# Five of eleven pairs of row tiles of each down product by Strassen's algorithm as well

## The chip, the cores and the metric

One core of a Trainium2 chip. The metric is the device time in microseconds of one execution of the whole program, the median of several runs. Matrix products run on TensorE (PE), elementwise work on VectorE (DVE) and ScalarE (ACT), a little on GpSimd (POOL); nearly all DMAs are issued by SyncE (SP), whose queue is worked through in order.

## The reference

Two decoder layers over 512 tokens of width 1024, in fp32. Each layer has two feed-forward blocks (FFN), so there are four:

```python
D_MODEL = 1024
D_FF = 2816
def swiglu(x, w_gu, w_down):
    gate, up = jnp.split(x @ w_gu, 2, axis=-1)
    return (jax.nn.silu(gate) * up) @ w_down
# per layer
#   h += 0.5 * post(SwiGLU_1(pre(h)))
#   h += post(concat(A, B, C) @ W_out)          "mix"
#   h += 0.5 * post(SwiGLU_2(pre(h)))
#   h += post((p[i] @ W_ple) * sigmoid(pre(h) @ W_gate))   "ple"
```

`pre` and `post` are RMS norms with gains. The down product is 512x2816 times 2816x1024.

## The kernel before

Every fp32 operand is split into two fp32r parts, hi (a cast, on ACT) and lo (operand minus hi, on DVE), and each product of two tiles is three matmuls into one PSUM bank: hi·hi, hi·lo, lo·hi (`mm3`, L252 to L254). So each weight tile of 128x1024 costs a load into `wst` (two buffers), an ACT cast `whi` (L143) and a DVE subtraction `wlo` (L140).

The gate/up product is already done by the Strassen–Winograd scheme: 7 products instead of 8 (`step`, L382; M1 to M7) for each of 11 pairs of row tiles, called mp 0 to 10 (mp 0 in the plain way). M4 of a pair is held back behind M2 of the next pair. From the products DVE and ACT assemble `c11`, `c12`, `c22`, then silu and product give g, whose last half is L455; g (128x1024: two row tiles of 512 tokens) goes to DRAM as `gd[mp]` (`store`, L406).

The down product then runs over k = 0 to 21, the 22 row tiles of 128 of the inner dimension. For each even k a pair of g is loaded back as `gl` (L543), cast to `gh` (ACT, L544) and reduced to its lo part (DVE, L545); for each k a weight tile is loaded and split. Then 4 token tiles t times 2 halves n times 3 matmuls of 128x512 go into the eight banks `acc[t, n]`, so all eight PSUM banks sum over the whole of k. The last TAIL = 4 values of k are done one token tile after the other. While t = 3 finishes, t = 0 and 1 go through `post_tile` (norm and residual; its DVE steps are L200, L199, L204) and `pre_tile` (the next norm, `v`, `hn` L228), and `turn` transposes them into `hT` (PE L234, ACT L237, DVE L238); t = 2 and 3 follow at the start of the next phase (`chains`), among its first weight splits (`wlo`, or `uw` in ple).

Each engine runs its instructions in the order in which the program has them; SP does so with its DMAs. A DMA into a buffer waits until the buffer's last reader is done, and all that stands behind it on SP waits too. Tiles called T, O, Q, U in the change and `gl`, `gh` share pools by tags: "u" and "s" and "x" of four buffers of 128x1024, "z" of five.

Of the kernel before, what the change touches and what calls it, by code (L numbers as in the profile page):

```python
# [21 lines left out]
P = 128  # L22
# [51 lines left out]
def kernel(ctx: ExitStack, tc: tile.TileContext, a: dict, out: bass.AP, phases=None):  # L74
# [210 lines left out]
    def ffn(l, w_gu, w_down, i, ends, hook):  # L285
# [140 lines left out]
        def step(mp, name, kind, w):  # L426
# [80 lines left out]
        held = (1, "M4", A22, w4)  # L507

        while True:
            prefetch(LOOK - len(queue))  # L510
            if not queue:
                break
            x = queue.pop(0)
            if x[:2] == (5, "M2"):
                hook(0)
            if x[1] == "M4" and x[0] < NMP - 1:
                held = x
                continue
            if x[1] == "M4":
                step(*held)  # L520
            step(*x)
# [4 lines left out]
        accs = {}  # L526
        ws, gs = {}, {}

        def down(t, k):
            for n in range(2):  # L530
                if not k:
                    accs[t, n] = ps(f"acc{t}{n}", ORD[t])
                mm3(accs[t, n][:], cut(gs[k], tsl(t)), ws[k](n * 512), k == 0, False)

        for k in range(KF):
            if k == 4:
                gpost, npre = ends()
            if k == 6:
                hook(1)
            ws[k] = load_w(w_down[k * P:(k + 1) * P, :])  # L540
            if k % 2 == 0:
                gl, gh = ut("gl", "z", F32R), ut("gh", "z", F32R)
                nc.sync.dma_start(gl[:].bitcast(F32), gd[k // 2][:])  # L543
                nc.scalar.copy(gh[:], gl[:].bitcast(F32))  # L544
                nc.vector.tensor_tensor(out=gl[:], in0=gl[:].bitcast(F32), in1=gh[:].bitcast(F32), op=ALU.subtract)  # L545
            gs[k] = tuple(x[:, (k % 2) * 512:(k % 2 + 1) * 512] for x in (gh, gl))
            if k < KF - TAIL:
                for t in range(NT):
                    down(t, k)
        def parts(t):  # L550
            return [accs[t, n][:] for n in range(2)]

        for t in range(NT):
            tail = [(n, k) for n in range(2) for k in range(KF - TAIL, KF)]
            if t == NT - 1:
# [802 lines left out]
```

## Time and profile before

| | |
|---|---|
| median of 3 runs | 2006.47 us (2005.75 to 2008.36) |
| profiled execution, its own time | 2007.29 us |
| its span in the trace | 2005.5 us (1.8 us lie outside) |
| granted TensorE clock, mean | 0.995 |
| PE busy | 1948.8 us, 97% |
| DVE busy | 1398.2 us, 70% |
| ACT busy | 925.4 us, 46% |
| first FFN: gate/up, down | 15.8 to 249.5 us, 249.5 to 371.5 us |

A busy PE is a PE that has matmuls in flight, and the duration of one matmul in a row is its time through the array; how fast matmuls follow each other is read from the starts of successive rows.

### The profile page before, as it was taken

What the parts mean: (1) busy time and instruction counts of PE and PEld (TensorE: products, weight loads), DVE (VectorE), ACT (ScalarE), POOL (GpSimd) and SP (SyncE); (2) the same over time, 40 slices, a digit from 0 to 9 for tenths busy, and PEclk for the clock granted to TensorE, in tenths of its full rate; (3) what the DMA queues carried; (4) which work ended last, traced back from release to release, by engine and by line L of the source; (5) the groups of instructions that cost most, each with busy time, mean ns of one, the idle gap of its engine ahead of it and who ended that gap; (6) DMA issues with size and microseconds to landing.
All of it is one profiled execution on the core that took longest, in us unless ns stands there. A gap on an engine that the chain in (4) does not pass through costs nothing.

```text
span 2005.5 us, 31044 instructions
## 1 busy us (share of the span) xinstructions
PE 1948.8 (97%) x12524; PEld 1754.2 (87%) x12524; DVE 1398.2 (70%) x2058; ACT 925.4 (46%) x1463; POOL 112.7 (6%) x135
## 2 busy tenths in 40 slices
PE   7999999999999999999999999999999999999988
PEld 6999988788689999887799999887877899998866
DVE  6887753669879888435688886346797798874364
ACT  4544433555545444324455444236545555443242
POOL 1000000113100000000000000001140000000000
PEclk9999999999999999999999999999998999999999
DMA  5543364323324342643253434443142244336431
GB/s 156 157 144 117 130 216 147 105 67 108 120 64 141 112 149 94 210 142 100 74 158 106 154 126 155 160 137 116 55 130 64 69 143 145 119 105 213 145 110 48
DMA packets 160609, 251.17 MB, mean 125 GB/s; under 512 B 11473, under 2 KB 116817, under 8 KB 160465
## 3 DMA queue, kind: packets, MB, share of 16 engines
q1 hardware_dynamic: 158160, 244.99, 38.0%
q10 hardware_dynamic: 2304, 4.20, 0.6%
q8 instruction: 98, 1.61, 0.3%
q14 instruction: 47, 0.38, 0.1%
HBM read 217.17 MB, written 29.36 MB: 123 GB/s over the span
## 4 chain that ended last, share of the span: by engine, by line
PE 79%; DVE 13%; ACT 3%; DMA 2%; issue 2%; POOL 1%; SPq 0%; DVEq 0%; ACTq 0%; POOLq 0%
PE X L382 21%; PE Z L382 11%; PE acc L254 8%; PE acc L252 8%; PE acc L253 8%; PE Y L382 5%; DVE wlo L140 2%; PE gate L253 1%; PE gate L254 1%; PE gate L252 1%; PE wo L252 1%; DVE A L321 1%; PE wo L254 1%; POOL r L181 1%; PE wo L253 1%
## 5 line engine op out<-in xcount | busy, mean ns | idle before, releaser
L337 ACT CAST whi<-wraw 128x1024 fp32r<-128x1024 f32 x280 | 291.9, 1050 | 342.1 <-issue 153.2
L140 DVE TENSOR_TENSOR wlo<-wraw,whi 128x1024 fp32r<-128x1024 f32 x280 | 339.7, 1221 | 93.5 <-ACT whi L337 93.1
L140 DVE TENSOR_TENSOR wlo<-wst,whi 128x1024 fp32r<-128x1024 f32 x150 | 183.2, 1222 | 150.5 <-ACT whi L143 150.0
L254 PE MATMUL acc<-whi,gl 128*128 128x512 f32 x704 | 274.5, 390 | 1.5 <-DVE gl L545 1.5
L252 PE MATMUL acc<-whi,gh 128*128 128x512 f32 x704 | 274.5, 390 | 0.0
L253 PE MATMUL acc<-wlo,gh 128*128 128x512 f32 x704 | 273.9, 389 | 0.0
L143 ACT CAST whi<-wst 128x1024 fp32r<-128x1024 f32 x150 | 157.4, 1050 | 212.5 <-PE acc L254 97.5
L382 PE MATMUL X<-hT,whi 128*128 128x256 f32 x1280 | 233.7, 283 | 0.0
L382 PEld LDWEIGHTS X<-hT,whi 128*128 128x128 f32 x1280 | 199.7, 192 | 0.0
L342 DVE TENSOR_TENSOR wraw<-wraw 128x1024 f32<-128x1024 f32 x160 | 195.4, 1222 | 3.4
L382 PE MATMUL X<-hT,wlo 128*128 128x256 f32 x640 | 181.1, 283 | 0.0
L254 PEld LDWEIGHTS acc<-whi,gl 128*128 128x128 f32 x704 | 132.1, 188 | 30.5 <-DVE gl L545 3.1
L253 PEld LDWEIGHTS acc<-wlo,gh 128*128 128x128 f32 x704 | 132.2, 188 | 27.2
L252 PEld LDWEIGHTS acc<-whi,gh 128*128 128x128 f32 x704 | 132.2, 188 | 27.0
L545 DVE TENSOR_TENSOR gl<-gl,gh 128x1024 fp32r<-128x1024 f32 x44 | 53.9, 1224 | 129.9 <-ACT gh L544 129.9
L181 POOL TENSOR_TENSOR r<-v,mhalf 128x1 f32<-128x1 f32 x64 | 39.8, 622 | 1693.4 <-DVE v L199 1594.9
L382 PEld LDWEIGHTS X<-hT,wlo 128*128 128x128 f32 x640 | 122.9, 192 | 0.0
L382 PE MATMUL Y<-hT,whi 128*128 128x256 f32 x640 | 117.1, 283 | 0.0
L544 ACT CAST gh<-gl 128x1024 fp32r<-128x1024 f32 x44 | 46.3, 1053 | 135.1 <-PE acc L253 119.7
L382 PEld LDWEIGHTS Y<-hT,whi 128*128 128x128 f32 x640 | 99.8, 192 | 0.0
L382 PE MATMUL Z<-S4h,wlo 128*128 128x256 f32 x320 | 91.0, 284 | 2.4 <-DVE wlo L140 2.4
L382 PE MATMUL X<-S2h,whi 128*128 128x256 f32 x320 | 90.8, 284 | 0.3 <-ACT c L437 0.3
(327 smaller groups left out, 4622.9 us busy)
## 6 DMA issues: line engine op xcount, KB each, us to landing
wraw<-in_ffn_gate_up_dram SPq DMA_DIRECT2D x160, 512.0 KB, 6.5
wst<-in_ffn_down_dram SPq DMA_DIRECT2D x88, 512.0 KB, 3.4
gl<-gd SPq DMA_DIRECT2D x44, 512.0 KB, 3.4
gd<-g SPq DMA_DIRECT2D x40, 512.0 KB, 3.2
wst<-in_w_in_dram SPq DMA_DIRECT2D x36, 512.0 KB, 3.8
gain<-in_norm_gains_dram SPq DMA_DIRECT2D x32, 256.0 KB, 5.7
wst<-in_ffn_gate_up_dram SPq DMA_DIRECT2D x16, 512.0 KB, 4.8
wst<-in_w_out_dram SPq DMA_DIRECT2D x16, 512.0 KB, 3.3
```

The lines of the kernel that those rows point to most:

```text
L140: newest["lo"] = eng.tensor_tensor(out=out_, in0=in_, in1=hi.bitcast(F32), op=ALU.subtract)
L143: newest["hi"] = nc.scalar.copy(out_, in_)
L181: nc.gpsimd.tensor_tensor(out=r, in0=v, in1=mhalf[:, :w], op=ALU.pow)
L252: pin(nc.tensor.matmul(acc, lh, rh, start=first, stop=False))
L253: pin(nc.tensor.matmul(acc, lh, rl, start=False, stop=False))
L254: pin(nc.tensor.matmul(acc, ll, rh, start=False, stop=last))
L321: nc.vector.tensor_tensor(out=out[:], in0=x[:], in1=y[:], op=op)
L337: nc.scalar.copy(hi[:], x[:])
L342: nc.vector.tensor_tensor(out=out[:], in0=x[:], in1=y[:], op=ALU.subtract)
L382: pin(nc.tensor.matmul(acc[:, m * 256:(m + 1) * 256], x[:, c], y, start=fresh and m == k == n == 0, stop=m == 1 and k == 3 and n == 2, ski ...
L544: nc.scalar.copy(gh[:], gl[:].bitcast(F32))
L545: nc.vector.tensor_tensor(out=gl[:], in0=gl[:].bitcast(F32), in1=gh[:].bitcast(F32), op=ALU.subtract)
```

## The change

FAST = [4, 5, 6, 7, 8]: these five of the eleven pairs of each down product are done by the Strassen–Winograd scheme, the other six as before. For such a pair the output 512x1024 is cut into quarters (C11 = banks `acc[0/1, 0]`, C12 = `acc[0/1, 1]`, C21 = `acc[2/3, 0]`, C22 = `acc[2/3, 1]`), the two g tiles and the two weight tiles into two halves each, and 7 products of 6 matmuls (`quarter`, `three`) take the place of 48 matmuls.

- In gate/up: after `store(mp)` of a fast pair, `sums` makes four sums of 128x256 of g on DVE and stores them to `gsum[mp]` in DRAM.
- Phase A, before all else of the down product: for each fast pair the two weight tiles e (in `wst`) and O (kept) and the loaded `ga` (one DMA from `gd`, one from `gsum`) are prepared (`prepare`: four DVE subtractions of 128x512, then the splits of `ga`, T and e), and four products, M6, M7, M1 and M5, go into C22, C21, C11 and C12: 24 matmuls for each pair. The first two pairs are prepared in the last part of gate/up.
- Between: U = M1 + M6 and CC = C21 + U + C12 are taken out of the banks (2 ACT copies, 6 DVE additions of 128x512). C11, C21 and C12 go on summing.
- Phase B: the other three products of each pair, 18 matmuls, from O, Q and the rest of g (`gb`).
- The plain pairs, 12 values of k; C22 starts anew. At the end `parts` adds U and CC into the banks ahead of `post_tile`: one DVE addition in place for t = 0 and 1 each, two for t = 2 and 3.

```diff
+    FAST = [4, 5, 6, 7, 8]
...
+        def sums(mp, G):
+            x = wpool.tile([P, 1024], F32, tag="wst", name="gsum", bufs=WST)
+            s2, s3, s1, s4 = (x[:, j * 256:(j + 1) * 256] for j in range(4))
+            a11, a21, a12, a22 = (G[:, j * 256:(j + 1) * 256] for j in range(4))
+            for o, y, z, op in ((s1, a21, a22, ALU.add), (s2, s1, a11, ALU.subtract), (s3, a11, a21, ALU.subtract), (s4, a12, s2, ALU.subtract)):
+                nc.vector.tensor_tensor(out=o, in0=y, in1=z, op=op)
+            pin(nc.sync.dma_start(gsum[mp][:], x[:]))
...
+        def load(j):
...
+            e = wpool.tile([P, 1024], F32, tag="wst", name="wst", bufs=WST)
+            pin(nc.sync.dma_start(e[:], w_down[2 * mp * P:(2 * mp + 1) * P, :]))
+            pin(nc.sync.dma_start(kept["O"][j][:], w_down[(2 * mp + 1) * P:(2 * mp + 2) * P, :]))
...
+        def load_ga(j):
+            mp = FAST[j]
+            gas.append(load_g([(slice(0, 256), gd[mp][:, :256]), (slice(256, 1024), gsum[mp][:, :768])]))
...
+        def prepare(j):
...
+            for x, y, z in ((t1, b12, b11), (t2, b22, t1), (b12, b22, b12), (q, b21, t2)):
+                nc.vector.tensor_tensor(out=x, in0=y, in1=z, op=ALU.subtract)
+            ready.append((split_g(*gl), split(t), split(e)))
...
+        for j in range(len(FAST)):
+            if j == len(ready):
+                prepare(j)
+            if 2 <= j < len(FAST) - 1:
+                load(j + 1)
+                load_ga(j + 1)
+            ga, wt, we = ready[j]
+            m1 = (C11, ga, 0, we, 0, not j)
+            todo = [(C22, ga, 1, wt, 1, not j), (C21, ga, 2, we, 1, not j)]
+            todo = [m1] + todo if j == len(FAST) - 1 else todo + [m1]
+            if j == 1:
+                prepare(2)
+            for x in todo + [(C12, ga, 3, wt, 0, not j)]:
+                quarter(*x, j == len(FAST) - 1)
...
+        for j, mp in enumerate(FAST):
+            gb = split_g(*load_g([(slice(0, 512), gd[mp][:, 512:]), (slice(512, 768), gsum[mp][:, 768:])]))
+            wo_ = split(kept["O"][j])
+            if j % 2 == 0:
+                wq = split(kept["Q"][j // 2], slice(0, 512 * min(2, len(FAST) - j)))
+            quarter(C11, gb, 0, wo_, 0, False)
+            quarter(C21, gb, 1, wq, j % 2, False)
+            quarter(C12, gb, 2, wo_, 1, False)
...
-        for k in range(KF):
-            if k == 4:
+        for u, k in enumerate(KS):
+            if u == 0:
                 gpost, npre = ends()
...
         def parts(t):
+            for n in range(t < 2, 2):
+                nc.vector.tensor_tensor(out=accs[t, n][:], in0=accs[t, n][:], in1=(U, CC)[t > 1 and n][t % 2], op=ALU.add)
             return [accs[t, n][:] for n in range(2)]
```

The first place is SP's queue around the start of the first down product. Before, the store of the last g (`gd10`) has weight tiles for the next k behind it, then the third pair of g:

```order
L189 DMA gain021_2912<-in_norm_gains_dram 128x512 [waits DMAHW0_49]
L406 DMA gd10_227<-g_2684 128x1024 [waits DMAHW1_49,DVE_49]
L161 DMA wst_2926<-in_ffn1_down_dram 128x1024 [waits DMAHW2_49,Activation_49]
L161 DMA wst_2961<-in_ffn1_down_dram 128x1024 [waits DMAHW3_49,Activation_49]
L543 DMA gl_2932<-gd2_219 128x1024 [waits DMAHW4_49,DMAHW1_49]
L676 DMA lmst_2998<-in_c_lmask_dram 128x448 [waits DMAHW5_49]
```

Now e and O of the third fast pair stand ahead of that store, and behind it stands that pair's `gl` in two parts, whose buffer is read by PE until the first fast pair's four products are done; e, O and `gl` of the fourth pair and e of the fifth are queued behind this load:

```order
L538 DMA wst_2829<-in_ffn1_down_dram 128x1024 [waits DMAHW4_49,Activation_49]
L539 DMA O_2726<-in_ffn1_down_dram 128x1024 [waits DMAHW5_49,PE_49]
L790 DMA lmst_3270<-in_c_lmask_dram 128x448 [waits DMAHW6_49]
L408 DMA gd10_227<-g_2719 128x1024 [waits DMAHW7_49,DVE_49]
L561 DMA gl_2860<-gd6_223 128x256 [waits DMAHW0_49,PE_49,Activation_49]
L561 DMA gl_2860<-gs6_230 128x768 [waits DMAHW1_49]
L538 DMA wst_2934<-in_ffn1_down_dram 128x1024 [waits DMAHW2_49,Activation_49]
L539 DMA O_2727<-in_ffn1_down_dram 128x1024 [waits DMAHW3_49]
L561 DMA gl_2937<-gd7_224 128x256 [waits DMAHW7_49,DMAHW4_49]
L561 DMA gl_2937<-gs7_231 128x768 [waits DMAHW5_49]
L538 DMA wst_2979<-in_ffn1_down_dram 128x1024 [waits DMAHW6_49,DVE_49]
```

What moved: four loads for each pair where there were three, and a load that waits for PE now has the next pair's weight tiles behind it.

The second place is DVE's queue there. Before, between the last gate/up instructions (L455 is the last half of g) DVE has one subtraction for each weight tile and one for each pair of g:

```order
L545 TENSOR_TENSOR gl_2774<-gl_2774,gh_2775 128x1024
L455 TENSOR_TENSOR g_2497<-sg_2736,c22_2437 128x2x256
L140 TENSOR_TENSOR wlo_2879<-wst_2876,whi_2878 128x1024
L455 TENSOR_TENSOR g_2684<-sg_2764,c22_2628 128x2x256
L545 TENSOR_TENSOR gl_2847<-gl_2847,gh_2848 128x1024
L140 TENSOR_TENSOR wlo_2929<-wst_2926,whi_2928 128x1024
L140 TENSOR_TENSOR wlo_2964<-wst_2961,whi_2963 128x1024
L677 CAST lmask_2997<-lmst_2998 128x448
L682 CAST spans_3001<-spst_3002 128x512
L545 TENSOR_TENSOR gl_2932<-gl_2932,gh_2933 128x1024
```

Now the second fast pair's splits, the last g (L466), and then for the third fast pair four subtractions (L555), the splits of T (`T_2722`) and e (`wst_2829`), the cast of a mask, and the split of `gl`:

```order
L567 TENSOR_TENSOR gl_2754<-gl_2754,gh_2818 128x1024
L555 TENSOR_TENSOR T_2722<-wst_2829 128x512
L555 TENSOR_TENSOR T_2722<-O_2726,T_2722 128x512
L555 TENSOR_TENSOR wst_2829<-O_2726,wst_2829 128x512
L555 TENSOR_TENSOR Q_2729<-O_2726,T_2722 128x512
L140 TENSOR_TENSOR wlo_2903<-T_2722,whi_2902 128x1024
L140 TENSOR_TENSOR wlo_2907<-wst_2829,whi_2906 128x1024
L791 CAST lmask_3269<-lmst_3270 128x448
L567 TENSOR_TENSOR gl_2860<-gl_2860,gh_2899 128x1024
L555 TENSOR_TENSOR T_2723<-wst_2934 128x512
L555 TENSOR_TENSOR T_2723<-O_2727,T_2723 128x512
L555 TENSOR_TENSOR wst_2934<-O_2727,wst_2934 128x512
```

What moved: for every pair of phase A seven DVE instructions stand where a pair of the loop before had three for twice the matmuls.

The third place is DVE's queue at the end of the second FFN, where ple's first weight splits (`uw`) follow on the transposed tiles `hT` of t = 0 and 1. Before:

```order
L225 TENSOR_SCALAR v<-ss 128x1
L228 SCALAR_TENSOR_TENSOR hn<-h,r,gain_8570 128x512
L228 SCALAR_TENSOR_TENSOR hn<-h,r,gain_8572 128x512
L238 TENSOR_TENSOR hT_8574<-ptr,hT_8574 128x512 x2
L140 TENSOR_TENSOR uw<-wst,uw 128x1024 x2
L200 SCALAR_TENSOR_TENSOR tmp<-acc_8455,gain_8566 128x512
L199 TENSOR_SCALAR v<-ssq 128x1
```

Now the additions into the banks (L664) stand between them; the last two are those of t = 3 and write the banks that its last matmuls fill:

```order
L228 SCALAR_TENSOR_TENSOR hn<-h,r,gain_8985 128x512
L228 SCALAR_TENSOR_TENSOR hn<-h,r,gain_8987 128x512
L664 TENSOR_TENSOR acc_8637<-acc_8637,U 128x512
L238 TENSOR_TENSOR hT_8989<-ptr,hT_8989 128x512 x2
L664 TENSOR_TENSOR acc_8638<-acc_8638,U 128x512
L664 TENSOR_TENSOR acc_8639<-acc_8639,U 128x512
L140 TENSOR_TENSOR uw<-wst,uw 128x1024 x2
L200 SCALAR_TENSOR_TENSOR tmp<-acc_8636,gain_8981 128x512
```

What moved: the `uw` splits stand behind two additions that wait for the last down matmuls.

## Rows read from the trace of the kernel before

**Rows 1.** The page, parts 1 and 4: busy time by engine, and the chain that ended last.
```profile
PE 1948.8 (97%) x12524; PEld 1754.2 (87%) x12524; DVE 1398.2 (70%) x2058; ACT 925.4 (46%) x1463; POOL 112.7 (6%) x135
...
PE 79%; DVE 13%; ACT 3%; DMA 2%; issue 2%; POOL 1%; SPq 0%; DVEq 0%; ACTq 0%; POOLq 0%
```

**Rows 2.** Windows of the first FFN: length, busy us (x count) by engine, PEclk, DMA share, GB/s.
```profile
15.80:249.50 233.70, 230.53 (x1892) 229.28 (x1893) 193.52 (x198) 115.90 (x146) 1.44 (x3) 1.00 0.43 134
249.50:275.00 25.50, 25.50 (x115) 21.11 (x114) 17.30 (x42) 11.67 (x15) 0.00 (x0) 1.00 0.67 236
275.00:300.00 25.00, 25.00 (x112) 20.71 (x111) 12.05 (x13) 8.74 (x9) 0.00 (x0) 1.00 0.60 210
```

**Rows 3.** Timeline of PE, second FFN's end and ple's start: start us, us, engine, line, operation.
```profile
925.83 0.39 PE L252 MATMUL acc<-whi,gh 128*128 128x512 f32 x1
...
934.44 0.40 PE L254 MATMUL acc<-whi,gl 128*128 128x512 f32 x1
...
937.40 0.40 PE L254 MATMUL acc<-whi,gl 128*128 128x512 f32 x1
...
939.92 0.48 PE L253 MATMUL gate<-uw,hT 128*128 128x512 f32 x1
```

**Rows 4.** Waits of PE over the span: us in total, times, longest us.
```profile
PE pj L252 <- ACT uwh L143: 3.2, 2, 1.6
...
PE acc L254 <- DVE gl L545: 1.5, 4, 0.4
```

**Rows 5.** Groups of DVE by line and form: busy us, mean ns, idle before.
```profile
L140 DVE TENSOR_TENSOR wlo<-wst,whi 128x1024 fp32r<-128x1024 f32 x150 | 183.2, 1222 | 150.5 <-ACT whi L143 150.0
...
L943 DVE TENSOR_TENSOR Ql<-qp,E 128x128 f32<-128x128 f32 x112 | 35.4, 376 | 0.1
L449 DVE TENSOR_TENSOR g<-c,c 128x512 f32<-128x512 f32 x40 | 27.6, 691 | 1.1
```

**Rows 6.** Timeline of DVE in one pair of the first gate/up product.
```profile
136.64 0.68 DVE L455 TENSOR_TENSOR g<-sg,c 128x512 f32<-128x512 f32 x1
138.42 1.23 DVE L140 TENSOR_TENSOR wlo<-wraw,whi 128x1024 fp32r<-128x1024 f32 x1 [1.10 <-ACT whi L337]
...
143.24 0.69 DVE L448 TENSOR_TENSOR c<-Z,c 128x512 f32<-128x512 f32 x1
143.97 0.69 DVE L449 TENSOR_TENSOR g<-c,c 128x512 f32<-128x512 f32 x1
...
146.97 0.68 DVE L451 TENSOR_TENSOR c<-X,c 128x512 f32<-128x512 f32 x1
147.57 1.21 DVE L342 TENSOR_TENSOR wraw<-wraw 128x1024 f32<-128x1024 f32 x1
148.71 1.22 DVE L140 TENSOR_TENSOR wlo<-wraw,whi 128x1024 fp32r<-128x1024 f32 x1
```

**Rows 7.** Timeline of PE there: the first matmuls of two products that follow each other.
```profile
137.21 0.28 PE L382 MATMUL X<-S2h,whi 128*128 128x256 f32 x1
...
140.09 0.28 PE L382 MATMUL Z<-S4h,whi 128*128 128x256 f32 x1
```

**Rows 8.** Timeline of SP's queue in the first down product: an issue of g's load.
```profile
275.41 0.38 SPq L543 DMA_DIRECT2D gl<-gd  x1
```

**Rows 9.** DMA issues: count, KB each, median us from issue to landing.
```profile
wraw<-in_ffn_gate_up_dram SPq DMA_DIRECT2D x160, 512.0 KB, 6.5
...
gl<-gd SPq DMA_DIRECT2D x44, 512.0 KB, 3.4
```

**Rows 10.** Group of ACT: the cast of the loaded g.
```profile
L544 ACT CAST gh<-gl 128x1024 fp32r<-128x1024 f32 x44 | 46.3, 1053 | 135.1 <-PE acc L253 119.7 <-DMA gd<-g 12.1 <-DMA gl<-gd 3.0
```

**Rows 11.** Timeline of DVE at the end of the second FFN (ple follows).
```profile
935.93 1.29 DVE L238 TENSOR_TENSOR hT<-ptr,hT 128x512 fp32r<-128x512 f32 x2 [3.10 <-ACT hT L237]
937.37 2.36 DVE L140 TENSOR_TENSOR uw<-wst,uw 128x1024 fp32r<-128x1024 f32 x2
```

**Rows 12.** Timeline of DVE at the end of the first FFN (mix follows).
```profile
371.39 1.29 DVE L238 TENSOR_TENSOR hT<-ptr,hT 128x512 fp32r<-128x512 f32 x2
```

More of the change, by code (lines that the diff above doesn't have):

```diff
@@ L456, in step @@
                 store(mp, d["G"])
+                if mp in FAST:
+                    sums(mp, d["G"])
         def mp1(name, w):
@@ L520, in ffn @@
                 step(*held)
+                prepare(1)
+                load(2)
+                step(*x)
+                load_ga(2)
+                continue
             step(*x)
@@ L525, in ffn, with three @@
         ORD = {0: "pt", 1: "pg", 2: "pm", 3: "pm"}
-        accs = {}
+        accs = {(t, n): ps(f"acc{t}{n}", ORD[t]) for t in (2, 3, 0, 1) for n in range(2)}
+        C11, C12, C21, C22 = ([accs[t, n] for t in ts] for ts in ((0, 1), (2, 3)) for n in range(2))
+        def three(acc, lhs, rhs, first, last):
+            (lh, ll), (rh, rl) = lhs, rhs
+            for x, (u, v) in enumerate(((lh, rh), (lh, rl), (ll, rh))):
+                pin(nc.tensor.matmul(acc, u, v, start=first and not x, stop=last and x == 2, skip_group_check=True))
@@ new lines, in quarter @@
+        def quarter(c, ga, ja, w, jw, start, stop=False):
+            for e in range(2):
+                three(c[e][:], cut(ga, slice(ja * 256 + e * P, ja * 256 + e * P + P)), cut(w, slice(jw * 512, jw * 512 + 512)), start, stop)
+        for j in range(len(FAST)):
[8 more added lines that the diff above has]
+            todo = [m1] + todo if j == len(FAST) - 1 else todo + [m1]
+            if j == 1:
+                prepare(2)
+            for x in todo + [(C12, ga, 3, wt, 0, not j)]:
+                quarter(*x, j == len(FAST) - 1)
@@ new lines, in ffn @@
+        U, CC = ([x[:, :512], x[:, 512:]] for x in kept["U"])
+        for e in range(2):
+            nc.scalar.copy(U[e], C11[e][:])
+            nc.vector.tensor_tensor(out=U[e], in0=C22[e][:], in1=U[e], op=ALU.add)
+        for e in range(2):
+            nc.vector.tensor_tensor(out=CC[e], in0=C21[e][:], in1=U[e], op=ALU.add)
+        for e in range(2):
+            nc.vector.tensor_tensor(out=CC[e], in0=C12[e][:], in1=CC[e], op=ALU.add)
+        wq = {}
+        for j, mp in enumerate(FAST):
[6 more added lines that the diff above has]
+            quarter(C12, gb, 2, wo_, 1, False)
@@ L527, in ffn @@
         ws, gs = {}, {}
+        KS = [2 * mp + x for mp in range(NMP) if mp not in FAST for x in range(2)]
         def down(t, k):
             for n in range(2):
-                if not k:
-                    accs[t, n] = ps(f"acc{t}{n}", ORD[t])
-                mm3(accs[t, n][:], cut(gs[k], tsl(t)), ws[k](n * 512), k == 0, False)
-        for k in range(KF):
-            if k == 4:
+                three(accs[t, n][:], cut(gs[k], tsl(t)), ws[k](n * 512), k == KS[0] and t > 1 and n == 1, False)
```

52 lines of the change are left out of this document (41 added, 11 removed).

## The prediction

> **What bounds the kernel now.** I read the page first: PE is busy for 97% of the span and makes up 79% of the chain that ended last, DVE is busy for 70% [rows 1]. Then the windows by stage: in the first FFN, PE is busy in the whole of 249.5 to 300 us, at a granted clock of 1.00, while DVE works 17.30 of the first 25.5 us and 12.05 of the next 25 [rows 2]. The list of PE's waits has one entry for the down products, `acc` on the lo part of g: 1.5 us over four FFNs [rows 4]. So each matmul taken out of a down product is worth its step, as long as the others remain fed, and what I have to look for is a new wait.
>
> **What is removed.** A fast pair has 7 products of 6 matmuls, 42, where the plain way has 48: 6 x 5 pairs x 4 FFNs = 120 matmuls fewer. A row gives 0.39 us for one, but that is its way through the array; the starts at 925.83 and 934.44 us have 38 steps between them, 8.61 / 38 = 0.2266 us [rows 3]. 120 x 0.2266 = 27.2 us. Matmuls of 128x512 into the eight banks remain what they were, so I keep that step for the new ones.
>
> **What is added in gate/up.** Four sums of 128x256 on DVE for each fast pair. No row has that shape; 0.38 us for 128x128 and 0.69 for 128x512 bound it [rows 5], four cost 1.5 to 2.8 us, and by the straight line between the two 1.9. [...] They stand right behind `g` (L455). There DVE now idles for 1.10 us, since the next `wlo` waits for its cast [rows 6], so some 0.8 us of the four push what follows back. DVE is busy 193.52 of 233.7 us in gate/up [rows 2], 40 us free over 11 pairs, and such a weight split waits for a buffer that PE has just left, with the buffers of the products in between still ahead of it. I cost it at nothing; if that cover were gone, it would be 0.8 x 20 pairs = 16 us. The 20 stores to `gsum` are small beside a DMA share of 0.43 there [rows 2].
>
> **Phase A, the main loss.** Take T as the start of the first fast product in an FFN. PE does a pair in 24 x 0.2266 = 5.44 us. DVE does for each pair four subtractions of 128x512 and three splits of 128x1024. A row alone says 0.69 and 1.22 us [rows 5], but DVE starts the next instruction sooner: 0.60 after a 128x512 one (146.97 to 147.57), 1.14 after a 128x1024 one (147.57 to 148.71), and 0.73 when the second reads the first's result, as L449 does L448's (143.24 to 143.97) [rows 6]. T2 reads T1, so a pair is 0.73 + 3 x 0.60 + 3 x 1.14 = 5.95 us, half a us more than PE has. In the plain loop it was three splits in 10.88 us.
>
> Now the order on DVE. The last but one `g` comes behind its M4; the last M4 (24 matmuls, 140.09 - 137.21 = 2.88 us [rows 7]) stands between that and T, so with ACT's silu and the multiplication that `g` ends near T - 1.3. Then: four subtractions and two splits of pair 1 (4.81) to T + 3.5; the last `g` (0.60) to T + 4.1; the split of pair 1's g (1.14) to T + 5.25, due at 5.44 + 0.45 = 5.9 (the third matmul is the first to read it). No wait. Pair 2: the same 4.81 to T + 10.1, or 10.5 in the first FFN with the mask's cast. Its `gl` is the piece that is late: the load has to wait for pair 0's last matmul at T + 5.44, its two parts take SP some 0.4 us each to issue [rows 8], and it lands 3.4 us [rows 9] behind the start or the end of the second issue, at T + 9.3 to 9.8; ACT's cast (1.05 [rows 10]) and DVE's split make T + 11.6 to 12.1, due at 10.88 + 0.45 = 11.3. So PE waits 0.3 to 0.8 us. From there DVE is the slower engine: pair 3 costs 5.95 - 5.44 = 0.5 us, and pair 4 0.5 + 0.2, since it begins with M1, which reads e's lo half, the last of its splits, with its second matmul. Sum 1.5 to 2.0 us; I take 1.8 for an FFN, 7.2 for four.
>
> Bounds: with `gl` in time DVE alone holds PE up by 0 + 0.4 + 0.7 = 1.1 (4.4 for four). The other end is the 6.5 us that four weight loads in a row take to land [rows 9]: `gl` is split at T + 14.7 to 15.2, the wait 3.4 to 3.9, with the later pairs 4.8 in all (19 for four). I stay near the low end because the loads at that place are the ones of 3.4 us, one pair at a time. Queued behind that waiting load on SP are e and O of pair 3, its g, and e of pair 4; they are issued at T + 6.5 to 8 and land before DVE comes to them at T + 12.
>
> [...] The rows just read show the next DVE instruction 1.14 us after the start of one that takes 1.21. [...]
>
> **Between, phase B, plain part.** U and CC are 2 copies on ACT and 6 additions on DVE, some 4 us, while PE does the 18 matmuls of 4.1 us from buffers split beforehand; DVE's work in phase B is two or three splits for each pair, 2.0 to 3.1 us for 4.1 on PE. Nothing. The setup work on DVE that made 249.5 to 275 us so full moves into the plain part, where DVE has 12.05 of 25 us [rows 2]. The loads of the plain part wait on nothing new. If one split were late here, it would cost about 1 us an FFN, as at phase A.
>
> **Ends.** Six additions of 128x512 into the banks, 0.60 to 0.69 us each. Towards ple: DVE begins the `uw` splits at 937.37, right behind `hT`, and the last down matmul starts at 937.40 [rows 3, 11]. Now two additions that need that matmul stand ahead: it ends at 937.80, so the splits begin near 937.8 + 0.65 = 938.45, 1.1 us later. PE's gate product reads their results from 939.92 [rows 3], and the first split would end at 939.7: just hidden. But all of DVE's work on t = 2 and 3 stands behind the splits, and PE waits in ple as it is (`pj`, twice up to 1.6 us [rows 4]), so later work passes the delay on, in part: 0 to 1.2, I take 0.9. Towards mix the same additions stand ahead of t = 2's `v` and `tmp`, right behind `hT` (371.39) [rows 12]: they add 1.2 us to a chain of norm, transposition and product, of which PE may see 0.2 to 2; I take 1.1. Two of each: 2 x 0.9 + 2 x 1.1 = 4 us (0.4 to 6.4).
>
> **Sum.** 27.2 - 7.2 - 4.0 = 16.0 us. The profiled execution took 2007.3 us, 0.8 above the median of 2006.5; less 16 it is 1991.3, and as a median 1990.5.
>
> **Rivals.**
> (a) All covers hold: phase A is fed in time because loads and DVE run closer than in my layout, and the ends see nothing. Gain 24 to 27 us, 1979.5 to 1982.5. For it speaks that PE hardly waits in the down products now [rows 4]; against it the 5.95 us of DVE against 5.44 of PE. Chance 0.10.
> (b) Phase A is held up more: `gl` lands late (6.5 us), 27.2 - 19 - 4 = 4 us gained, 2002; half-way between that and my case 10 us, 1996. Here belongs DVE in steps of its full row times: 0.45 us more for each of four pairs, 1.8 for an FFN, 7 in all, 1997.5. [...] The 1.10 us gap filled badly in gate/up (up to 16 us lost) leads to the same region. Chance together 0.22.
> (c) Slower: SP's queue. The load of pair 2's `gl` waits for PE, and if e and O of pair 3 behind it land so late that DVE stands still again at each pair, the loss repeats with every pair. It breaks even when an FFN loses (27.2 - 4) / 4 = 5.8 us, that is with landings about 4 us longer than 3.4. With 7.5 us an FFN it is 27.2 - 30 - 4 = 7 slower, 2013. For it: 6.5 us exists in this trace, and the DMA share is already 0.67 there [rows 2]. Against it: that is for four weight loads at once. Chance 0.05.
> (d) It doesn't do what it says: the six matmuls saved for each pair are given back by a longer step, since four quarters now follow each other in two banks at a time. No row speaks for it; the trace has only the present order. 2002 to 2010. Chance 0.05.
> My case, 1984 to 1996, has 0.58.
>
> **How the numbers follow.** The time is that of the likeliest, 1990.5, with its own range 1984 to 1996 from the bounds of phase A and the ends. For eight in ten the range reaches from 1981.5 (half of (a) in) to 2000 (most of (b) in; its late end, (c) and (d) left out, some 0.19 with the rest of (a)). A measurement of this kernel tells about 0.2%, 4 us, from no change: faster by more 0.88 (my case, (a), most of (b), a little of (d)), same 0.07, slower 0.05.
>
> **What would show it.** 120 matmuls fewer on PE, and 27 us less busy time, at the same step; PE waits for DVE `gl`, `wlo` of e in phase A of about 2 us in each FFN, in pairs 2 to 4; the `uw` splits about 1 us behind `hT` towards ple; no wait in gate/up. Wrong it would be by waits for casts or DMAs in gate/up, by a step over 0.23 us in phases A and B, or by landings of `gl` over 5 us.

## The result and the profile after

The changed kernel takes 1985.66 us (median of 4 runs, 1983.64 to 1989.87) where the kernel before, on the same chip, takes 2007.41: a ratio of 0.9898, 95% interval 0.9887 to 0.991. Forecast were 1990.5 us, in a range from 1981.5 to 2000, and faster with a chance of 0.88. The profiled execution took 1986.0 us, 21.3 less than that of before; its span is 1984.1 us, its mean granted clock 0.995, the same.

The page, parts 1, 4 and 6 (busy us, share and count by engine; the chain that ended last; DMA issues with KB each and us to landing), answers to [rows 1, 9]:

```profile
PE 1924.9 (97%) x12404; PEld 1730.3 (87%) x12404; DVE 1549.3 (78%) x2318; ACT 976.9 (49%) x1525; POOL 111.3 (6%) x135
...
PE 74%; DVE 16%; DMA 3%; ACT 3%; issue 2%; POOL 1%; SPq 1%; DVEq 0%; POOLq 0%; ACTq 0%
...
gl<-gd SPq DMA_DIRECT2D x24, 512.0 KB, 4.2
...
O<-in_ffn_down_dram SPq DMA_DIRECT2D x20, 512.0 KB, 5.8
```

There are 120 matmuls fewer and 23.9 us less of busy PE (27 were forecast); DVE has 151 us more, ACT 51.5. Of the chain, PE has 74% instead of 79, DVE 16 instead of 13.

The windows of the changed kernel by stage tell where the time went. They are cut at the first matmul of gate/up, the first of the down product and the start of its last one; what follows is mix (after FFN 1 and 3) or ple (after 2 and 4). Columns as in [rows 2]:

```profile
15.83:248.94 233.11, 230.71 (x1893) 229.44 (x1893) 201.58 (x223) 113.69 (x144) 1.36 (x3) 1.00 0.45 146
248.94:366.54 117.60, 115.98 (x515) 94.56 (x514) 89.09 (x128) 62.32 (x83) 2.20 (x4) 1.00 0.56 192
366.54:582.45 215.91, 208.32 (x1116) 169.40 (x1115) 168.43 (x458) 115.97 (x264) 40.19 (x41) 1.00 0.28 87
...
810.26:926.92 116.66, 115.15 (x508) 93.74 (x506) 75.60 (x88) 52.05 (x67) 2.20 (x4) 1.00 0.51 173
926.92:995.90 68.98, 63.41 (x291) 50.85 (x289) 47.67 (x72) 34.61 (x70) 6.44 (x10) 0.98 0.30 97
...
1344.74:1561.66 216.92, 209.72 (x1117) 170.50 (x1115) 168.60 (x458) 115.96 (x264) 40.62 (x41) 0.99 0.27 86
...
1908.22:1976.20 67.98, 62.93 (x274) 49.45 (x272) 38.34 (x57) 26.76 (x52) 4.79 (x7) 0.95 0.25 85
```

The same cuts in before; three of its rows, and then all lengths side by side:

```profile
249.53:371.46 121.93, 121.56 (x545) 100.50 (x544) 61.49 (x92) 46.05 (x65) 2.21 (x4) 1.00 0.50 170
371.46:588.54 217.08, 208.38 (x1116) 169.57 (x1115) 166.71 (x453) 115.50 (x263) 41.08 (x41) 1.00 0.28 85
...
1359.85:1581.97 222.12, 214.05 (x1116) 173.39 (x1115) 167.02 (x453) 115.42 (x263) 41.05 (x41) 0.97 0.27 83
```

| us | before, four FFNs | after | difference |
|---|---|---|---|
| gate/up | 233.68, 227.79, 231.57, 227.80 | 233.11, 227.81, 231.38, 228.40 | -0.1 |
| down | 121.93, 121.07, 121.94, 121.08 | 117.60, 116.66, 117.46, 118.16 | -16.1 |
| mix, ple | 217.08, 68.94, 222.12, 66.75 | 215.91, 68.98, 216.92, 67.98 | -5.1 |

The down products give 16.1 of the 27.2 us that 120 matmuls are worth. The other 5.1 us come from stages in which the change does only a few additions; there the forecast had a loss of 4. Most of these 5.1 us lie in the second mix (222.12 against 216.92), which shows a granted clock of 0.97 before and 0.99 after; the part on the prediction comes back to this.

**Where 11 us of the down products stay.** Phase A of the second FFN begins at T = 810.26. The timeline of DVE there (start us, us, engine, line, operation, in brackets the idle time before and its releaser) answers to [rows 6]:

```profile
814.29 1.22 DVE L567 TENSOR_TENSOR gl<-gl,gh 128x1024 fp32r<-128x1024 f32 x1
...
816.75 0.68 DVE L555 TENSOR_TENSOR wst<-O,wst 128x512 f32<-128x512 f32 x1
817.35 0.68 DVE L555 TENSOR_TENSOR Q<-O,T 128x512 f32<-128x512 f32 x1
818.01 1.22 DVE L140 TENSOR_TENSOR wlo<-T,whi 128x1024 fp32r<-128x1024 f32 x1
819.15 1.22 DVE L140 TENSOR_TENSOR wlo<-wst,whi 128x1024 fp32r<-128x1024 f32 x1
821.36 1.23 DVE L567 TENSOR_TENSOR gl<-gl,gh 128x1024 fp32r<-128x1024 f32 x1 [1.00 <-ACT gh L566]
822.50 0.68 DVE L555 TENSOR_TENSOR T<-wst 128x512 f32<-128x512 f32 x1
...
828.45 0.68 DVE L555 TENSOR_TENSOR T<-wst 128x512 f32<-128x512 f32 x1
```

Pair 1's `gl` is split by 815.5, T + 5.25, as laid out. DVE then stands still for 1.00 us, for the cast of pair 2's `gl`, and its split ends at T + 12.3 (forecast: T + 11.6 to 12.1). From 822.50 to 828.45 is one pair in 5.95 us, the forecast's number to the hundredth. The timeline of PE shows what each late piece costs (three places: pairs 2, 3 and 4), to be read against the step of [rows 3]:

```profile
821.72 0.40 PE L605 MATMUL acc<-wlo,gh 128*128 128x512 f32 x1
822.64 0.50 PE L605 MATMUL acc<-whi,gl 128*128 128x512 f32 x1 [0.53 <-DVE gl L567]
822.98 0.40 PE L605 MATMUL acc<-whi,gh 128*128 128x512 f32 x1
...
828.01 0.39 PE L605 MATMUL acc<-wlo,gh 128*128 128x512 f32 x1
828.58 0.50 PE L605 MATMUL acc<-whi,gl 128*128 128x512 f32 x1 [0.18 <-DVE gl L567]
828.92 0.40 PE L605 MATMUL acc<-whi,gh 128*128 128x512 f32 x1
...
833.75 0.39 PE L605 MATMUL acc<-whi,gh 128*128 128x512 f32 x1
834.52 0.50 PE L605 MATMUL acc<-wlo,gh 128*128 128x512 f32 x1 [0.39 <-DVE wlo L140]
```

From 821.72 to 822.64 are 0.92 us where a step is 0.2266, and the step behind it, 822.64 to 822.98, is 0.34: each stop costs a further 0.11 us that no list of waits has. What PE waits for at these places, as a list for this phase A:

```profile
PE acc L605 <- DVE gl L567: 0.7, 2, 0.5
PE acc L605 <- DVE wlo L140: 0.4, 1, 0.4
```

It gives 1.1 us. Adding up, from the starts in the trace, what each step is above 0.2266 gives 2.35, 2.25, 2.22 and 2.06 us for the four phases A, 8.9 in all, and besides once 1.7 us in the fourth FFN, where the first `gl` of the plain part landed some 7 us behind its issue. Before, the down products have 2.41, 1.52, 2.40 and 1.52 us of such excess at their ends; after, the same. With 0.5 us left over, that is the difference between 27.2 and 16.1.

**The ends.** The timelines of PE and DVE where ple begins (second FFN) answer to [rows 3, 11]:

```profile
926.92 0.39 PE L605 MATMUL acc<-whi,gl 128*128 128x512 f32 x1
```
```profile
926.67 1.37 DVE L664 TENSOR_TENSOR acc<-acc,U 128x512 f32<-128x512 f32 x2
927.95 2.35 DVE L140 TENSOR_TENSOR uw<-wst,uw 128x1024 fp32r<-128x1024 f32 x2
```

The `uw` splits begin 1.03 us behind the start of the last down matmul where they were 0.03 ahead of it: 1.06 us later, as forecast. The stage itself is 68.98 us long instead of 68.94.

### The profile page after: what moved, and what is told of

Its sections match the earlier page's. It is cut to its first block, busy times and chain, and to the rows that moved or that the text cites. A ratio compares the mean times of both kernels' runs of the same rounds, so it can differ in the third digit from the quotient of the medians.

```text
span 1984.1 us, 31432 instructions
## 1 busy us (share of the span) xinstructions
PE 1924.9 (97%) x12404; PEld 1730.3 (87%) x12404; DVE 1549.3 (78%) x2318; ACT 976.9 (49%) x1525; POOL 111.3 (6%) x135
## 4 chain that ended last, share of the span: by engine, by line
PE 74%; DVE 16%; DMA 3%; ACT 3%; issue 2%; POOL 1%; SPq 1%; DVEq 0%; POOLq 0%; ACTq 0%
PE X L384 22%; PE acc L605 18%; PE Z L384 11%; PE Y L384 5%; DVE wlo L140 3%; DMA wraw<-in_ffn_gate_up_dram 1%; PE gate L253 1%; PE gate L254 1%; PE gate L252 1%; DVE A L322 1%; PE wo L252 1%; PE wo L254 1%; PE wo L253 1%; DVE hT L238 1%; DVE wraw L343 1%
## 5 line engine op out<-in xcount | busy, mean ns | idle before, releaser
L605 PE MATMUL acc<-whi,gl 128*128 128x512 f32 x664 | 260.0, 392 | 4.9 <-DVE gl L567 4.9
L605 PE MATMUL acc<-wlo,gh 128*128 128x512 f32 x664 | 259.0, 390 | 1.7 <-DVE wlo L140 1.7
L605 PE MATMUL acc<-whi,gh 128*128 128x512 f32 x664 | 259.7, 391 | 0.8 <-ACT gh L566 0.6
L140 DVE TENSOR_TENSOR wlo<-wst,whi 128x1024 fp32r<-128x1024 f32 x130 | 158.5, 1221 | 79.3 <-ACT whi L143 78.9
L143 ACT CAST whi<-wst 128x1024 fp32r<-128x1024 f32 x110 | 115.3, 1049 | 118.7 <-PE acc L605 44.4
L605 PEld LDWEIGHTS acc<-whi,gl 128*128 128x128 f32 x664 | 124.6, 188 | 36.0 <-DVE gl L567 10.5
L605 PEld LDWEIGHTS acc<-wlo,gh 128*128 128x128 f32 x664 | 124.7, 188 | 28.8 <-DVE wlo L140 3.4
L605 PEld LDWEIGHTS acc<-whi,gh 128*128 128x128 f32 x664 | 124.7, 188 | 27.7 <-ACT gh L566 2.6
L567 DVE TENSOR_TENSOR gl<-gl,gh 128x1024 fp32r<-128x1024 f32 (+1 forms) x64 | 72.8, 1137 | 68.0 <-ACT gh L566 67.8
L566 ACT CAST gh<-gl 128x1024 fp32r<-128x1024 f32 (+1 forms) x64 | 63.0, 985 | 98.4 <-PE acc L605 70.2
```

Of the source, the lines that this page charges most:

```text
L140: newest["lo"] = eng.tensor_tensor(out=out_, in0=in_, in1=hi.bitcast(F32), op=ALU.subtract)
L143: newest["hi"] = nc.scalar.copy(out_, in_)
L566: nc.scalar.copy(gh[:, w_], gl[:, w_].bitcast(F32))
L567: nc.vector.tensor_tensor(out=gl[:, w_], in0=gl[:, w_].bitcast(F32), in1=gh[:, w_].bitcast(F32), op=ALU.subtract)
L605: pin(nc.tensor.matmul(acc, u, v, start=first and not x, stop=last and x == 2, skip_group_check=True))
```

## The experiments

Two theories stood at the start. **One:** phase A costs what DVE's work costs (5.95 us a pair against PE's 5.44) and what one late load adds, and the ends cost some us. **Rival:** the loss hangs on something else, loads or a chain over several engines, and the ends cost nothing. The ratio given beside a time is to executions of the kernel before.

**The changed kernel and the kernel before, once more.** No edit.

> The changed kernel once more, as the measure for the other three. Both theories: 0.9898 of before, some 1986 us, and again about 2.3 us of gaps of TensorE beyond its step in phase A of each FFN (pairs 2, 3 and 4 of the five). If the second ple stage or the second mix stage shows a lower granted clock in one of the profiles and not in the other, the stages of single profiles are worth several us less than they seem.

1985.58 us, 0.9894 (0.9879 to 0.9909), and the down products 117.44, 116.74, 117.59, 117.02: 17.2 us less than before, without the one late load of the fourth FFN.

> The kernel before once more, for a second profile. If the second mix stage is 222 us again with a granted clock below 1, the lower clock there belongs to that kernel's course and its absence after the change is part of the gain; if it is near 217 like the first, the 5 us of the first profile are one execution's.

2006.55 us. The down products are within 0.05 us of the first profile, stage by stage, gate/up within 0.6 us; mix is 219.84 and 218.36 where it was 217.08 and 222.12. So the mix stages vary by some us from one execution to the next in one and the same kernel, and the down products do not.

**The price of the 120 matmuls: no subtractions, early loads.** The four subtractions of each pair are left out (T and Q are replaced by O, so its output differs), pair 2's `gl` has a buffer of its own and is loaded early, O of pair 3 too, and the first `gb` is split ahead of U.

```diff
-            for x, y, z in ((t1, b12, b11), (t2, b22, t1), (b12, b22, b12), (q, b21, t2)):
-                nc.vector.tensor_tensor(out=x, in0=y, in1=z, op=ALU.subtract)
-            ready.append((split_g(*gl), split(t), split(e)))
+            ready.append((split_g(*gl), split(o), split(e)))
...
-                step(*x)
                 load_ga(2)
+                load_o(3)
+                step(*x)
```

> Leaves out the four subtractions of each fast pair (O takes the place of T and Q, so the products are others), with gl and O of the third and fourth pair loaded early as in best_o, and the first gb split ahead of U and CC. VectorE then has 3.4 us a pair. My theory: no gaps in phase A at all; a down stage is 9 us less the ends' own gaps: 27.2 us less than before over the four. In time 1977 at the changed kernel's clock. Rival (a lower clock takes back what phase A gains): the down stages shrink as said, the time stays at 1982 or above.

1975.03 us, 0.9846 (0.9832 to 0.9861). The down products take 116.29, 114.26, 115.13 and 114.24, 459.9 us: 26.1 less than before; the missing 1.1 us is nearly all in the first FFN, where one weight split (`wlo`, 0.8) and one `gl` (0.2) of the plain part come late. PE waits nowhere in phase A. So the 27.2 us are real, and phase A holds 9 to 10 us of them back in the changed kernel (26.1 against the 16.1 and 17.2 of its two profiles).

**The late load of pair 2.** Its `gl` goes into another pool and is issued one product earlier; U takes that buffer later.

```diff
-            gas.append(load_g([...]))
+            gas.append(load_g([...], "zzxzz"[j]))
...
-                step(*x)
                 load_ga(2)
+                step(*x)
...
+        kept["U"] = [ut("U", "x") for _ in range(2)]
```

> The third fast pair's gl goes into a buffer of another pool that is free before phase A, and its load stands ahead of the last store of g. My theory (pair 2's wait is the late gl, those of pairs 3 and 4 are VectorE's 5.95 us a pair against TensorE's 5.44): the 1.2 us of gaps at pair 2 go, those of pairs 3 and 4 stay (0.5 and 0.7), 1.2 us less an FFN, some 4.5 us in all, near 1981.5. Rival (all three waits follow from SP's queue, whose loads all come behind that one): all 2.3 us go, 9 us, near 1977. Third: nothing, since VectorE comes to that gl no sooner: 1986.

1985.12 us, 0.9889 (0.9875 to 0.9903); down 116.61, 116.21, 116.99, 116.27, together 466.1, 3.8 less than in the changed kernel's profile and 2.7 less than in the second. The stop at pair 2 is gone; those at pairs 3 and 4 have grown from 0.5 and 0.7 to 0.6 to 1.2 and 0.7 to 1.4 us. DVE's timeline shows what is late next:

```profile
824.22 0.69 DVE L554 TENSOR_TENSOR T<-O,T 128x512 f32<-128x512 f32 x1 [0.53 <-DMA O<-in_ffn_down_dram]
```

**Less work on DVE.** The fourth subtraction (Q, needed in phase B only) of pairs 3 and 4 is moved behind phase A, 0.6 us less for DVE in each of those pairs; the first `gb` is split ahead of U.

```diff
+            subs = ((t1, b12, b11), (t2, b22, t1), (b12, b22, b12), (q, b21, t2))
+            if j > 2:
+                late[j] = subs[3]
+            for x, y, z in subs[:3 if j > 2 else 4]:
...
+            if j + 2 in late:
+                x, y, z = late[j + 2]
+                with behind((last,)):
+                    nc.vector.tensor_tensor(out=x, in0=y, in1=z, op=ALU.subtract)
```

> The subtraction Q of pairs 3 and 4 is made in phase B, where it is first read; the first gb is split ahead of U and CC by order. Loads as in the changed kernel. My theory: VectorE has 0.6 us less for pair 3 and 1.2 less up to pair 4, so the gaps at pairs 3 and 4 go (1.2 us an FFN, 4.5 us in all, near 1981.5) and pair 2's stay. Rival (SP's queue holds all three pairs): no change, 1986.

1985.98 us, 0.9892 (0.9874 to 0.9909); down 117.89, 116.73, 117.57, 116.50. The stops at pairs 3 and 4 are what they were. DVE's timeline says why:

```profile
824.67 0.68 DVE L558 TENSOR_TENSOR T<-wst 128x512 f32<-128x512 f32 x1
...
827.20 1.22 DVE L140 TENSOR_TENSOR wlo<-T,whi 128x1024 fp32r<-128x1024 f32 x1 [0.51 <-ACT whi L338]
...
830.62 0.68 DVE L558 TENSOR_TENSOR T<-wst 128x512 f32<-128x512 f32 x1
```

The pair still takes 5.95 us (824.67 to 830.62). The place of Q is now a wait for ACT's cast of T, which can begin only when the second subtraction is done, and ends where Q would have ended. So theory one's reason does not suffice for pairs 3 and 4: a pair is as long as the chain of two subtractions, cast and three splits, and DVE's sum of work is just as long, so that shortening the sum alone gains nothing.

**Subtractions alone left out.** As the first of these, but with the loads where the change has them; the output differs in the same way.

> The same four subtractions left out, but the loads as in the changed kernel; the first gb split ahead of U and CC. My theory: pair 2's gap of about 1 us stays, since its gl is late, and those of pairs 3 and 4 go: 1.2 us an FFN. Rival (pairs 3 and 4 wait for loads, not for the chain on VectorE and ScalarE): they stay at 0.5 and 0.7.

1984.22 us, 0.9894 (0.9878 to 0.9911), at a granted clock of 0.992 to 0.995; down 116.59, 115.09, 116.61, 115.31. The stops at pairs 3 and 4 are gone, that at pair 2 remains; the list of PE's waits for the second FFN's phase A has one entry:

```profile
PE acc L603 <- DVE gl L565: 0.5, 1, 0.5
```

So pair 2 is the load, and pairs 3 and 4 hang on the subtractions, which this kernel takes out of the chain and out of DVE's sum alike; the two do not explain each other.

**Both mended.** The early load and the moved Q together, as in the two diffs above; then also O of pair 3 ahead of the last store of g.

> Both edits together. My theory: the two parts add, 2.3 us an FFN go, 9 us in all, near 1977. Rival of SP's queue: no more than gl_early alone. If phase B now waits (for Q or the first gb), part of it is given back there.

1986.91 us, 0.9899 (0.9885 to 0.9913); down 117.80 (with 1.1 for one late `wlo` of the plain part), 116.11, 117.08, 116.07.

> best_late, and the second weight tile O of pair 3 is loaded ahead of the last store of g (in gl_early VectorE waited 0.5 us for it in one phase A, as it landed 7 us after its issue). My theory: pair 2 has no gap, pairs 3 and 4 keep the 0.5 and 0.7 of the chain T1, T2, cast, splits: 1.2 to 1.4 us of gaps an FFN instead of 2.3, all four FFNs alike. In time that is 4 us less than the changed kernel at the same granted clock (1982); if the stretches of lower clock in the mix stages that best_late showed in all its executions (clock 0.992 to 0.994 against 0.995 to 0.997) belong to an earlier end of the down product, they take that back: 1986. Rival (loads in general): gaps of pair 3 still vary by 0.5 us.

```diff
                 load_ga(2)
+                load_o(3)
                 step(*x)
```

1983.79 us, 0.9889 (0.9874 to 0.9903); down 116.71, 115.07, 116.91, 115.83, 464.5 us in all: 4.3 and 5.4 us less than in the changed kernel's two profiles. In three of four FFNs pairs 2 and 3 have no stop left; pair 4 keeps 0.7 to 1.5 us. The whole is no faster than the changed kernel by what these times alone can tell: granted clocks of 0.991 to 0.995 (mean 0.9930) stand against a mean of 0.9957 over nine executions of the changed kernel. By the price of the clock worked out below, some 1.0 us for 0.001, that would be near 3 us, which is more than half of what the down products gained.

**The chain cut.** On top of the early load and the moved Q, T's two subtractions of the next pair stand ahead of this pair's last split, that of e, so that ACT can cast while DVE splits; for this the loads and the preparation of pairs 3 and 4 also stand earlier in the program.

```diff
+            g, t = split_g(*gas[j]), split(kept["T"][j % 2])
+            tsubs(j + 1)
+            hi, lo = w_pair()
+            nc.scalar.copy(hi[:], loads[j][:])
+            with behind((done[j + 1],)):
+                split_lo(lo[:], loads[j][:], hi[:])
```

> As best_late, but VectorE makes T1 and T2 of the next pair ahead of this pair's last split. In q_late, Q's 0.6 us became idle time: VectorE waited for ScalarE's cast of T, which waits for T2, so the 5.95 us of a pair are the chain T1, T2, cast, three splits and not VectorE's busy time. My theory now: with T1 and T2 made early a pair takes VectorE 5.35 us, less than TensorE's 5.44, and the gaps of phase A shrink from 2.3 to some 0.5 us an FFN; the down stages go from 117 to near 115.2 us, 7 us in all. Rival (the weight pairs' five buffers, or the loads, hold pairs 3 and 4): the gaps at pairs 3 and 4 stay above 0.5 each.

1990.91 us, 0.9921 (0.9905 to 0.9937), against the expectation; down 120.43, 116.99, 119.43, 117.74. DVE's waits in the second FFN:

```profile
DVE T L557 <- DMA wst<-in_ffn_down_dram: 1.6, 1, 1.6
DVE wlo L140 <- ACT whi L338: 0.6, 1, 0.6
DVE T L557 <- DMA O<-in_ffn_down_dram: 0.4, 1, 0.4
```

What is late is now a load into `wst`, for the fifth pair. That it starts late because the split that moved back is the last reader of its buffer follows from the order of the program, and SP's queue in the trace agrees (it waits 6.3 us for a `wlo` split and issues the load at 827.78, as that split ends); no run tried it with another buffer. (In the first FFN, 3.4 us of phase A also ran at half clock.) Cutting one chain lengthened another, so no run here shows what the chain costs by itself.

**The sums in gate/up.** Left out: the four sums of each fast pair; g itself is stored in their place.

```diff
-            for o, y, z, op in ((s1, a21, a22, ALU.add), ...):
-                nc.vector.tensor_tensor(out=o, in0=y, in1=z, op=op)
-            pin(nc.sync.dma_start(gsum[mp][:], x[:]))
+            pin(nc.sync.dma_start(gsum[mp][:], G[:]))
```

> Leaves out the four sums of 128x256 in gate/up; g itself is stored in their place, so the products of the fast pairs are others. By the prediction: no change (1986), the gate/up stages within 0.5 us of the changed kernel's. Rival: up to 16 us less, if VectorE's time there is on the path.

1987.06 us, 0.9906 (0.9892 to 0.992); gate/up 234.10, 227.97, 231.28, 228.97. Nothing is gained: the sums are hidden.

**The additions at the ends.** Left out: the six additions of U and CC into the banks.

```diff
-            for n in range(t < 2, 2):
-                nc.vector.tensor_tensor(out=accs[t, n][:], in0=accs[t, n][:], in1=(U, CC)[t > 1 and n][t % 2], op=ALU.add)
```

> Leaves out the six additions of U and CC into the banks of each FFN, so three of the four quarters of the output lack a part. By the prediction's term for the ends: 4 us less than the changed kernel (0.4 to 6.4), 1982. By the traces (the stages after the down products are no longer than before): within 1 us an end, and within 2 us in all.

1991.3 us, 0.9924 (0.991 to 0.9938): not faster without them but 5.6 slower. Down is as in the changed kernel (117.84, 116.97, 117.81, 117.02); the two mix stages are 219.97 and 219.37, 6.5 us longer. The trace gives two reasons. The waits of PE around the start of the first mix are those of before again (compare the two lists in the next section):

```profile
PE ptr L234 <- DVE hn L228: 1.9, 2, 1.2
PE ptr L234 <- DVE hT L238: 0.5, 1, 0.5
```

With the additions PE has 38 matmuls of mix ahead of its first transposition of t = 2, without them 33, as in before; that is worth 1.1 us a mix, 2.2 of the 6.5. The other reason is the granted clock: by the trace's record of it, PE has half the clock for 6.8 us in each of the two mix stages, where the changed kernel's first mix has none and its second 3.4 us. So the additions cost no time towards mix; they save some.

**Two fast pairs instead of five.** Both are prepared in gate/up: 48 matmuls fewer than before, nothing for phase A to wait for. The first `gb` is split ahead of U and CC, as in some of the kernels above.

```diff
-    FAST = [4, 5, 6, 7, 8]
+    FAST = [7, 8]
```

> Only two fast pairs (7 and 8), both prepared before phase A; the first gb split ahead of U and CC. By the prediction's price of a matmul: 48 fewer, 10.9 us less than before, and no gaps in phase A; ends as in the changed kernel. 1995.7 by the prediction's step alone; with 4 us for the ends 1999.7; if the ends gain 4 us, as the changed kernel's stages seem to, 1991.7.

1998.01 us, 0.9959 (0.9947 to 0.9971); down 121.65, 119.71, 120.58, 119.80, together 481.7: only 4.3 us less than before, where 48 steps are 10.9. The list of PE's waits in the second FFN:

```profile
PE acc L603 <- DVE U L629: 0.6, 1, 0.6
PE acc L603 <- DVE gl L567: 0.2, 1, 0.2
```

The stops, 1.2 to 2.4 us an FFN with the slow steps behind them and 6.4 in all, now stand at the beginning of phase B; phase A has none. Work for U, CC and the first `gb` that no stop betrays with five pairs is bare with two; I read it as the missing cover of three pairs on PE, which no run tried apart.

## Why the prediction was right, point by point

- **The sum, 16.0 us, measured 21.3 in the profiles and 21.8 in the medians.** The time lies in the range, but that it lies there is in part luck: two terms are wrong in opposite directions and partly cancel. Phase A and the plain part lose more than forecast (10.6 us, with 0.5 left over, in place of 7.2), the ends gain about 1.5 where they should have lost 4.0, and the clock adds to the gain.
- **Removed, 27.2 us: right.** Without the waits of phase A 26.1 us appear, and 1.0 of the rest is what came late in the first FFN's plain part.
- **Gate/up at nothing: right.** The stages sum to 0.1 us less, and leaving the sums out gains nothing. One sum takes 421 ns, not the 0.48 us of the straight line, as the groups of DVE by form have it (the first 40 of 80):

```profile
L416 DVE TENSOR_TENSOR gsum<-g 128x256 f32<-128x256 f32 x40 | 15.2, 421 | 0.7
```
- **Phase A, "DVE is the slower engine", 7.2 us: mis-sized, and in part for a wrong reason.** It measures 8.9 us. DVE's layout is right to 0.1 us, and pair 2's `gl` is late by the load, as said: the kernel without subtractions keeps that stop alone, the early load removes it. Its second part lands at T + 9.7 to 10.0, where 9.3 to 9.8 was laid out. Two things were missing. Each stop also costs a slow step behind it (0.34 us for 0.2266), and at pair 2 PE in three of four FFNs waits for ACT's cast `gh` of the same load as well, 0.1 to 0.3 us, before it waits for the lo part: about 0.9 to 1.2 us in place of 0.3 to 0.8. And DVE's sum of work is not the whole cause at pairs 3 and 4: 0.6 us of it removed changed nothing, since the chain subtraction, subtraction, cast on ACT, splits is as long. It went unseen because the two lengths agree; that the chain alone would hold PE up as much is not shown.
- **Between, phase B and plain part at nothing: right but for one late load.** The first `gl` of the plain part in the fourth FFN cost 1.7 us, in the second profile 0.3 and a slow step of 0.1.
- **The rival that DVE steps by its full row times: out.** In the rows of after 128x512 is followed after 0.60 (816.75 to 817.35), 128x1024 after 1.14 (818.01 to 819.15), beside durations of 0.68 and 1.22: the next one starts 0.08 us ahead of the end. By full row times a pair would take 4 x 0.69 + 3 x 1.22 = 6.4 us; it took 5.95 (822.50 to 828.45).
- **Ends, a loss of 4.0 us: failed.** The delay is there (`uw` 1.06 us later; the norm of t = 2 towards mix 0.9 later), but the step that turned it into time of PE, "later work passes the delay on", did not hold towards mix. The list of PE's waits in the 34 us around the start of the first mix, of before and then of after:

```profile
PE ptr L234 <- DVE hn L228: 1.8, 2, 1.2
PE ptr L234 <- DVE hT L238: 0.5, 1, 0.5
```
```profile
PE sg L254 <- DVE hT L238: 0.8, 1, 0.8
PE ptr L234 <- DVE hn L228: 0.5, 2, 0.3
```

  2.3 us became 1.3. PE's timeline of before and then of after has the first transposition of t = 2 there, 8.47 us behind the last down matmul's start and 9.36:

```profile
379.94 1.29 PE L234 MATMUL ptr<-ident,hn 128*128 128x128 f32 x8 [0.58 <-DVE hn L228]
```
```profile
375.90 0.63 PE L234 MATMUL ptr<-ident,hn 128*128 128x128 f32 x4 [0.33 <-DVE hn L228]
```

  The forecast delayed DVE's norm and left PE's order as it was. But that order changed with the additions: five more matmuls stand ahead of the transposition, so PE comes to it later and waits less. The 90th matmul behind the last of the down product starts 21.8 to 22.1 us behind it in the mix stages of before with the full clock, and 20.9 us in all of the changed kernel; the kernel without additions has the old order and the old waits. So each mix gains 1.1 us where 1.1 were to be lost. Towards ple, where 0.9 was forecast for each, the first loses nothing (68.94 and 68.65 before, 68.98 and 68.74 after) and the second some 0.7 (66.7 and 66.8 before, 67.5 in the second profile of the changed kernel, all at the full clock).

- **In its place 5.1 us gained behind the FFNs**, which no step had. Some 1.6 of them are the 2.2 us of the two mix stages less the 0.7 of ple; the rest goes with TensorE's clock (last section). By the trace's record of it, PE has half the clock for 13.7 us of the second mix in the first profile of before, for 3.4 in its second profile (218.36 us) and for 3.4 in both profiles of the changed kernel (216.92 in each).
- **What the clock is worth in the whole time.** Over 31 executions of before its mean is 0.9939, over 9 of the changed kernel 0.9957. Within one kernel an execution with 0.001 less takes longer by 1.1 us (a straight line through the 31) or 0.9 (through the 9), so I estimate 1.0 us for 0.001 and near 2 us for the difference. The mean times of the same executions, 2006.9 and 1986.1, differ by 20.8; with 2 taken out some 19 are left, of which the down products are 16.1 and 17.2 in the two profiles and the ends about 1.6. In part the higher clock may come from the change: three of the six mix stages profiled without the additions show half the clock some 18 us behind their start, just behind a wait of PE of 1.2 us that is 0.2 with the additions, and none of the 22 with them does. Whether all of it does is not settled.
- **The rivals.** (a) all covers hold and (b) phase A costs 10 us more than said: neither, though the down products lie 1.7 us (phase A) to 3.4 us (with the late load) on the side of (b). (c) SP's queue: its mechanism exists, O and `gl` land late once the first stop is mended, at 0.3 to 0.7 us of DVE's time and not at 4. (d) a longer step: out, 0.2266 holds wherever nothing is late.

## What to carry to other kernels

A matmul taken out of a stage that PE bounds was worth its step here (26.1 of 27.2 us where nothing held phase A up), and what came back was found by following the one piece that is late in each round, its cast on the other engine included: taking 0.6 us of work off DVE gained nothing where a chain over DVE and ACT was as long. Price a stop at more than its wait in the list: the step behind it took 0.34 us for 0.2266. A delay on a feeding engine need not become a loss (towards mix the norm of t = 2 came 0.9 us later, and each mix was 1.1 us shorter, since PE came to it later as well), so read the new order of the engine that is fed. And before a gain is explained, compare the stages that the change does not touch: here they moved by as much as a term of the sum, from one execution to the next (the second mix 222.12 and 218.36 us in two profiles of before), and mostly with the granted clock in them.

## What the runs showed of the hardware

By the trace's record TensorE's granted clock stands at one half for short stretches, and where it does differs between the profiles: in that of after for 3.4 us each in the first ple stage, the third gate/up and the second mix, for 6.8 in the second ple and for the last 2.6 of the span; in the first of before for 3.4 us in the third gate/up, for 3.4 and 10.2 in the second mix and for the last 3.8 of the span. The mix stages are longer with it: over all profiles, a mix of the changed kernel and its variants takes 215.8 to 216.1 us with no such stretch, 216.9 to 217.4 with 3.4 us at half clock, 219.4 and 220.0 with 6.8 (the kernel without the additions) and 219.1 to 219.7 with 10.2; so the time at half clock alone does not give the length. Windows of 10 us, from some 8 us behind the start of the first ple stage, of after and then of before (columns as above, PEclk third from the end):

```profile
935.00:945.00 10.00, 6.33 (x25) 3.89 (x24) 9.50 (x15) 6.38 (x13) 1.65 (x3) 0.95 0.50 163
945.00:955.00 10.00, 10.00 (x47) 8.28 (x46) 6.34 (x8) 5.28 (x6) 0.00 (x0) 0.88 0.67 222
```
```profile
945.00:955.00 10.00, 6.40 (x25) 3.97 (x25) 9.64 (x14) 7.11 (x15) 1.50 (x3) 1.00 0.51 153
955.00:965.00 10.00, 9.24 (x40) 6.56 (x41) 6.17 (x8) 4.92 (x6) 0.16 (x1) 1.00 0.72 213
```

PE is busy 6.33 of 10 us in the one and 6.40 in the other, and only the one sees a lower clock. The second profile of the changed kernel has no lower clock in this stage at all (68.74 us long, against 68.98 with 3.4 us at half clock in the first), so the kernel alone does not decide it. At the lower level PE's timeline of after shows a step of 0.43 us (944.97 to 945.40):

```profile
944.97 0.63 PE L252 MATMUL pj<-uwh,uw 128*128 128x512 f32 x1
945.40 0.63 PE L253 MATMUL pj<-uwl,uw 128*128 128x512 f32 x1
```

What decides it was not found. By the 1.0 us for 0.001 above, an estimate, mean clocks of 0.9957 and 0.9939 cost some 4 and 6 us an execution, as much as the best of the mended versions saved in the down products.
